# A two-layer decoder trunk on one core: transfers moved to SyncE, gates and transposes given precedence, and seven products in the last gate

## The chip, the core and the metric

The program runs on one core of a Trainium2 chip. A core has five engines, each with its own queue of instructions: TensorE (PE in the profile; its weight loads are PEld), VectorE (DVE), ScalarE (ACT), GpSimd (POOL) and SyncE (SP), which here only issues transfers between memory (HBM) and the core's SBUF. The metric is the device time of one execution in microseconds (us), as the median of several runs. All arithmetic is float32.

## The reference, cut to what matters

The input is h, 256 tokens by 2048 features. Two layers follow, each of the same outline:

```python
hn = rmsnorm(h, norm)
u = hn @ w_in                       # 2048 x 6144, then 2048 x 8208
y = token_mixers(u)                 # gated recurrences (layer 0), mLSTM (layer 1)
h = h + y @ w_out                   # output projection, 2048 x 2048
pl = rmsnorm(p[i] @ ple_w[i], ple_norm[i])
h = h + sigmoid(h @ ple_gate_w[i]) * pl      # the gate, 2048 x 2048
```

and a final `rmsnorm(h, final_norm)` gives the output. The change lies in the output projections and gates of both layers, and in what is loaded and stored around them.

## The kernel before, in words

**A matmul in three.** Every float32 weight tile (128 x 1024, 512 KB) is loaded by SyncE into one of five buffers named raw, and split: ScalarE writes a rounded copy whi (line 137 in `load_weights`, line 219 in `split_weights`), VectorE the rest, wlo = raw - whi (lines 138 and 220). There are four buffers of each. Activations are split the same way (ahl). A product is then three matmuls: high by high, high by low, low by high. Loads, copies and subtractions are written down in the order of the program; a scheduler orders each engine's queue by a priority, which is an instruction's place in the program less an offset (`high_priority`), among those that are ready by its own estimate. Splits have an offset of 400. `issue_after` puts an instruction behind another one of its engine.

**Projections.** With tokens as output rows, a weight matrix is done in chunks of 512 output features, each in four quarters of the 2048 inputs (`quarter_tok`, lines 199 to 213: 24 matmuls, both halves of the tokens, two weight tiles). `project_two` does two chunks interleaved, in the order of quarters (0,0), (0,1), (1,0), (1,1), (0,2), (1,2), (0,3), (1,3), so that the last features are needed late. `plain` is the same quarter in another form.

**Seven products.** `seven` (line 287) does a pair of chunks with one quarter of the inputs (two in some places) as a 2 x 2 block product in seven multiplications in place of eight (Strassen-Winograd). It needs sums of blocks of weights, added by VectorE in place (line 306) or by an accumulating transfer of GpSimd (line 310), and sums of blocks of activations (`combos`, line 247). The other quarters of the pair run as `plain`, between the products, in the order of a string: a and b are plain quarters of the first and second chunk, the digits are products, A and F hand over finished halves, and a dot is a pump. The output projections of both layers ("eo", "oo") and the first gate ("g0") do chunks 0 and 1 by `project_two` and then chunks 2 and 3 by `seven` (`two_and_seven`). The last gate ("g1") does chunks 0 and 1 by `project_two` (through `chunks`, with n = 3), chunk 2 by `project_tok` and chunk 3 by `last_chunk`, in which the second half of the tokens is done in two halves of columns, for a short end.

**What hangs on a finished chunk.** `out_proj` (line 588) adds a finished half to h (VectorE, line 595, offset 100). `ple_gate` (line 601) takes a tanh on ScalarE and two operations on VectorE (lines 608 to 610). Both then start `to_features` (line 553): two 32 x 32 block transposes on VectorE (line 558), a hop through memory issued by GpSimd (`across`, lines 677 and 680: one transfer out, four back), and the split of the features for the next projection (ahl). Such steps are generators in named lanes. Each plain quarter pumps once in its middle: every lane takes a step, and what it issues is put behind the latest instruction noted for its engine (`last`). `ready` runs a lane on until the features that a quarter needs exist.

**Transfers beside the weights.** After the first gate, h (four tiles of 512 KB) is spilled to memory by GpSimd (`spill`, line 1152: six pumps of waiting, then one tile at each), because its room is needed. Before the second output projection it is reloaded by GpSimd (`home`, line 1446: three pumps of waiting, then one tile at each); `out_proj` needs it there. The row of gains of the second layer's embedding norm is loaded by GpSimd in two halves (`row`, line 535), spread over all partitions; `ple_gain_squares` (line 1475) takes squares at its steps 0 to 3 and multiplies by the row at its steps 2 to 5. The row of the final norm is loaded in the same way at the second pump of the last gate.

Of the kernel before, what the change touches and what calls it, by code (L numbers as in the profile page):

```python
# [11 lines left out]
F32 = mybir.dt.float32  # L12
# [7 lines left out]
P = 128  # L20
# [25 lines left out]
def trunk(ctx: ExitStack, tc: tile.TileContext, a, out):  # L46
# [79 lines left out]
    def load_weights(src, pieces=(1, 1), halves=(0, 1), rooms=None):  # L126
        parts = []
        for hf in halves:
            raw = wp.tile([P, 1024], F32, name="raw", tag="raw", bufs=5)
            hi, lo = rooms(hf) if rooms else (wp.tile([P, 1024], F32R, name=n, tag=n) for n in ("whi", "wlo"))  # L130
            n = 1024 // pieces[hf]
            for c in range(0, 1024, n):
                r, h, l = (x[:, c:c + n] for x in (raw, hi, lo))
                sy.dma_start(out=r, in_=block(src, hf * 1024 + c, n))
                with ExitStack() as order:
                    order.enter_context(tc.high_priority(offset=400))
                    last["act"] = s.copy(h, r).ins  # L137
                    last["dve"] = v.tensor_tensor(out=l, in0=r, in1=h.bitcast(F32), op=ALU.subtract).ins  # L138
            parts.append((hi, lo))
        return parts  # L140
# [19 lines left out]
    def tokens(x, k, hf):  # L160
        return x[:, k, hf * P:(hf + 1) * P]

    def project_tok(w, j, act, before=None):

        ps = [pm.tile([P, 512], F32, name="mm", tag="mm") for _ in range(2)]
# [18 lines left out]
        for j in range(2, n):  # L184
            yield project_tok(w, j, act)

    def two_and_seven(w, act, before, where, places, home=None):

        qs = {}
        start("combos", combos(act, 0, qs, *where))  # L190
        for c, ps in enumerate(project_two(w, act, before)):
            for hf in range(2):
                yield c, hf, ps[hf]
        drain("combos")
        for b, hf, src in seven(w, 2, act, qs, (0,), *places(), home and home()):
            yield 2 + b, hf, src

    def quarter_tok(w, j, kq, act, ps):

        parts = load_weights(w[4 * j + kq])  # L200
        for hf in range(2):
            for kk in range(4):
                k = kq * 4 + kk
                hi, lo = parts[kk // 2]
                c = (kk % 2) * 512
                ah, al, _ = act[k // 2]
                xh, xl = (tokens(x, k % 2, hf) for x in (ah, al))
                wh, wl = hi[:, c:c + 512], lo[:, c:c + 512]
                te.matmul(ps[hf], xh, wh, start=(k == 0), stop=False)  # L209
                te.matmul(ps[hf], xh, wl, start=False, stop=False)  # L210
                last["pe"] = te.matmul(ps[hf], xl, wh, start=False, stop=(k == KT - 1)).ins  # L211
            if hf == 0:
                pump()

# [69 lines left out]
    def seven(w, j, act, qs, kqs, room, part, home=None, order=None, acc=None, before=None, third=None):  # L284
# [4 lines left out]
        def load(tile_of, b, side):  # L289
            tiles = []  # L290
            for kq in kqs:
                t = tile_of()
                sy.dma_start(out=t, in_=src(b, side, kq))
                tiles.append(t)
            return tiles

# [32 lines left out]
        E = px.tile([P, 512], F32, name="mx", tag="mx")  # L329
        A, F, B = (pm.tile([P, 512], F32, name="mm", tag="mm") for _ in range(3))  # L330
        b5, g = part(), part()
        X = load(room, 0, 0)
# [12 lines left out]
        if not acc:  # L345
            W = load(ring, 1, 0)
            add(Y, W)
            add(W, X)
        rows = [list(rest), list(rest)]
        did = set()  # L350
        for op in order or ORDERS[len(kqs)]:
            if op in "ab":
                b = "ab".index(op)
                kq = rows[b].pop(0)
                plain(w, j + b, kq, act, ((A, F), (E, B))[b], end=not rows[b])
            elif op == "5":
                product(B, combo(1), split(W))
                add(X, Y)
                if acc:
                    add_loaded(Y)  # L360
                keep(b5, B)
# [165 lines left out]
    def ple_norm(pls, pss, rp):  # L527
# [4 lines left out]
        v.tensor_scalar(rp, rsqrt_cols(total(pss, 4)), 0.5, None, op0=ALU.mult)  # L532
        yield

    def row(pool, tag, bufs, i):

        halves = []
        for b in range(2):
            t = pool.tile([P, 1024], F32, name="row", tag=tag, bufs=bufs)
            gp.dma_start(out=t, in_=a["rows"][i, b * 1024:(b + 1) * 1024].partition_broadcast(P))  # L540
            halves.append(t)
        return halves

    def ple_gain(pls, load):
        rows = load()
# [7 lines left out]
    def to_features(h, c, act, gain, name, more=None):  # L553

        w = room("w")
        w5 = w.rearrange("p (j c h t) -> p h c j t", j=4, c=4, h=2)
        for hf in range(2):
            v.transpose(w5[:, hf], h[:, hf].rearrange("p (c j q) -> p c j q", c=4, j=4))
        r = room("r")
        yield from across(w, r, f"d{name}{c}", 7 if c == 2 else 6)  # L560
        r5 = r.rearrange("p (i c h t) -> p c h i t", i=4, c=4, h=2)
# [23 lines left out]
                step(f"{lane}{kq}")  # L585
        return before

    def out_proj(hq, parts, lane):

        act = {}  # L590
        for c, hf, src in parts:
            drain("home")
            if src is not None:
                with tc.high_priority(offset=100):
                    v.tensor_tensor(out=hq[c][:, hf], in0=src, in1=hq[c][:, hf], op=ALU.add)
            if hf:
                start(f"{lane}{c}", to_features(hq[c], c, act, None, lane))
# [3 lines left out]
    def ple_gate(hq, parts, pls, rp, hss, gain, lane, more):  # L601

        nxt = {}
        for c, hf, src in parts:
            drain("pg")
            th = tp.tile([P, 512], F32, name="th", tag="th")
            h = hq[c][:, hf]
            s.activation(th, src, AF.Tanh, scale=0.5)
            v.scalar_tensor_tensor(th, th, 1.0, pls[c][hf], op0=ALU.add, op1=ALU.mult)
            v.scalar_tensor_tensor(h, th, rp[:, hf:hf + 1], h, op0=ALU.mult, op1=ALU.add)  # L610
# [572 lines left out]
    with tc.tile_pool(name="m1", bufs=2) as m1:  # L1183
# [260 lines left out]
        hq = []  # L1444

        def home():
            for _ in range(3):
                yield
            for c in range(4):
                t = hp.tile([P, 2, 512], F32, name="hq", tag="h")  # L1450
                gp.dma_start(out=t, in_=away[c])
                hq.append(t)
                yield

# [18 lines left out]
            v.tensor_scalar(rp, rsqrt_cols(total(pss, 4)), 0.5, None, op0=ALU.mult)  # L1473

        def ple_gain_squares():
            rows = row(m1, "vt", 6, 1)
            for g in range(6):
                for hf in range(2):
                    if g < 4:
                        squared(pls[g][hf], pss[:, g, hf:hf + 1])  # L1480
                    if g > 1:
                        pl = pls[g - 2][hf]
                        v.tensor_tensor(out=pl, in0=pl, op=ALU.mult,
                                        in1=rows[(g - 2) // 2][:, (g % 2) * 512:(g % 2 + 1) * 512])
                yield

        step("fm3")
# [4 lines left out]
        act = out_proj(hq, two_and_seven(a["oo"], y, ready(y, "fm"), (m1, "vt", 6), in_m1, lambda: hq[3][:, 0]), "fo")  # L1492
        drain("emb")


        hss = m1.tile([P, 5, 2], F32, name="hss", bufs=1)
# [14 lines left out]
                v.scalar_tensor_tensor(sq, pl, 1.0, pl, op0=ALU.mult, op1=ALU.mult, accum_out=o)  # L1511

        def final_rows():
            yield
# [4 lines left out]
        for g, ps in enumerate(chunks(a["g1"], 3, act, ready(act, "fo"))):  # L1519
            drain("fnr")  # L1520
            for hf in range(2):
                pl = pls[g][hf]
                gated(g, ps[hf], hq[g][:, hf], pl, hf)
                v.tensor_tensor(out=pl, in0=pl, in1=fnr[g // 2][:, (g % 2) * 512:(g % 2 + 1) * 512], op=ALU.mult)


        def last_chunk():
# [187 lines left out]
```

## Time and profile before

| what | us |
|---|---|
| median of 3 runs | 1023.46 (1023.36 to 1025.24) |
| the profiled execution | 1024.17 |
| its span, from the first instruction to the last | 1022.4 |

The granted clock of TensorE was 0.997 over the span. The kernel moves 242.66 MB at a mean of 237 GB/s. In the chain of waits, the stages lie about like this (start in us): output projection of layer 0, its seven products 343.5; first gate, its seven products 429.2; second output projection about 839, its seven products 883.1; last gate about 925; last matmul about 1013.

How to read the rows: a row of a timeline has the start, the duration, the engine, the line of the kernel, the operation, the tiles as out<-in, the shapes and how many instructions are merged (x2). The chain that ended last is followed back from the last instruction, and its rows have start, length and what it was. A row of the waits has who waited, for whom, and the total, the number and the longest. A row of stretches has the bounds, then the busy time of PE, PEld, DVE, ACT and POOL with their numbers of instructions, then the clock, the share of the DMA engines and GB/s. "SPq" is SyncE issuing; its duration in a merged row is the stretch over which it issued.

### The profile page before, as it was taken

The numbers are of one execution on the slowest core, as the hardware profiler recorded it, in microseconds if no ns is written. First come the engines' busy times: TensorE is split into PE (matmuls) and PEld (weight loads), VectorE is DVE, ScalarE is ACT, GpSimd is POOL, SyncE is SP. The second block draws the span as 40 slices with busy tenths as digits, with TensorE's granted clock in tenths as the row PEclk, the third lists the DMA queues.
The fourth block names the chain that finished last, engine by engine and source line by source line (L and its number), as shares of the span: only waits on it lengthen the run. The fifth ranks groups of instructions, "written<-read, shape, count | busy, mean of one in ns | idle before, by whom it ended". The sixth has DMA issues, their size and how long they took to land.

```text
span 1022.4 us, 14498 instructions
## 1 busy us (share of the span) xinstructions
PE 1011.1 (99%) x5164; PEld 838.4 (82%) x5164; DVE 828.8 (81%) x1216; ACT 654.0 (64%) x940; POOL 107.1 (10%) x192
## 2 busy tenths in 40 slices
PE   9999999999999999999999999999999999999996
PEld 8888888888888888887888888888888887888885
DVE  7858968969686888888669997888889996986783
ACT  7775554686974455666557878766667777554662
POOL 0111101011111112021012100000011112112000
PEclk9999999999999999999999999999999999999998
DMA  9987756567689799487789756566979789689652
GB/s 358 334 228 247 223 179 198 170 197 232 234 254 306 240 304 300 150 271 246 252 295 289 246 165 211 184 207 194 277 176 287 228 267 310 204 258 297 206 185 83
DMA packets 69817, 242.66 MB, mean 237 GB/s; under 512 B 9041, under 2 KB 10449, under 8 KB 69745
## 3 DMA queue, kind: packets, MB, share of 16 engines
q1 hardware_dynamic: 54576, 192.84, 57.0%
q0 software_dynamic: 14736, 48.38, 17.6%
q8 instruction: 40, 0.66, 0.3%
q10 hardware_dynamic: 432, 0.52, 0.1%
q14 instruction: 33, 0.26, 0.1%
HBM read 221.78 MB, written 19.92 MB: 236 GB/s over the span
## 4 chain that ended last, share of the span: by engine, by line
PE 95%; DMA 2%; DVE 1%; ACT 1%; issue 0%; POOL 0%; ACTq 0%; DVEq 0%; POOLq 0%
PE mm L233 25%; PE mm L209 15%; PE mm L210 15%; PE mm L211 15%; PE mx L233 7%; PE mx L211 3%; PE mx L210 3%; PE mx L209 3%; PE mm L509 1%; DMA row<-in_rows_dram 1%; PE nu L1339 1%; PE mx L509 1%; PE mm L1540 1%; PE mm L1539 1%; PE mm L1541 1%; DMA r<-dfg 1%
## 5 line engine op out<-in xcount | busy, mean ns | idle before, releaser
L138 DVE TENSOR_TENSOR wlo<-raw,whi 128x1024 fp32r<-128x1024 f32 (+1 forms) x313 | 375.9, 1212 | 115.2 <-ACT whi L137 109.0
L137 ACT CAST whi<-raw 128x1024 fp32r<-128x1024 f32 (+1 forms) x313 | 326.3, 1047 | 219.1 <-PE mm L211 100.0
L210 PE MATMUL mm<-wlo,ahl 128*128 128x512 f32 x704 | 274.3, 390 | 1.0 <-DVE wlo L138 1.0
L209 PE MATMUL mm<-whi,ahl 128*128 128x512 f32 x704 | 275.2, 391 | 0.0
L211 PE MATMUL mm<-whi,ahl 128*128 128x512 f32 x704 | 274.0, 389 | 0.0
L233 PE MATMUL mm<-whi,ahl 128*128 128x512 f32 x636 | 204.8, 390 | 0.0
L210 PEld LDWEIGHTS mm<-wlo,ahl 128*128 128x128 f32 x704 | 132.2, 188 | 28.6 <-DVE wlo L138 1.6
L209 PEld LDWEIGHTS mm<-whi,ahl 128*128 128x128 f32 x704 | 132.1, 188 | 28.0 <-issue 0.4
L211 PEld LDWEIGHTS mm<-whi,ahl 128*128 128x128 f32 x704 | 132.2, 188 | 27.4
L233 PEld LDWEIGHTS mm<-whi,ahl 128*128 128x128 f32 x636 | 119.4, 188 | 24.7
L233 PE MATMUL mm<-wlo,ahl 128*128 128x512 f32 x318 | 123.9, 390 | 0.0
L220 DVE TENSOR_TENSOR wlo<-ch,whi 128x1024 fp32r<-128x1024 f32 x62 | 74.8, 1219 | 11.5 <-ACT whi L219 10.4
L219 ACT CAST whi<-ch 128x1024 fp32r<-128x1024 f32 x62 | 64.7, 1049 | 20.9 <-PE mm L233 11.2
L233 PEld LDWEIGHTS mm<-wlo,ahl 128*128 128x128 f32 x318 | 59.7, 188 | 12.2
L209 PE MATMUL mx<-whi,ahl 128*128 128x512 f32 x160 | 62.2, 389 | 0.0
L210 PE MATMUL mx<-wlo,ahl 128*128 128x512 f32 x160 | 62.2, 389 | 0.0
L211 PE MATMUL mx<-whi,ahl 128*128 128x512 f32 x160 | 62.2, 389 | 0.0
L233 PE MATMUL mx<-whi,ahl 128*128 128x512 f32 x168 | 55.3, 390 | 0.0
L233 PE MATMUL mm<-whi,q 128*128 128x512 f32 x132 | 44.8, 390 | 0.0
L233 PEld LDWEIGHTS mx<-whi,ahl 128*128 128x128 f32 x168 | 31.5, 188 | 6.9 <-ACT xr L566 0.4
L209 PEld LDWEIGHTS mx<-whi,ahl 128*128 128x128 f32 x160 | 30.0, 188 | 6.3
L210 PEld LDWEIGHTS mx<-wlo,ahl 128*128 128x128 f32 x160 | 30.0, 188 | 6.2
(380 smaller groups left out, 1255.0 us busy)
## 6 DMA issues: line engine op xcount, KB each, us to landing
raw<-in_ew_dram SPq DMA_DIRECT2D x64, 512.0 KB, 5.0
raw<-in_g_dram SPq DMA_DIRECT2D x62, 512.0 KB, 4.8
raw<-in_oqk_dram SPq DMA_DIRECT2D x32, 512.0 KB, 5.5
raw<-in_eo_dram SPq DMA_DIRECT2D x30, 512.0 KB, 5.0
raw<-in_oo_dram SPq DMA_DIRECT2D x30, 512.0 KB, 5.5
raw<-in_ov_dram SPq DMA_DIRECT2D x29, 512.0 KB, 4.4
raw<-in_oog_dram SPq DMA_DIRECT2D x24, 512.0 KB, 4.3
raw<-in_oz_dram SPq DMA_DIRECT2D x20, 512.0 KB, 5.2
```

The source lines that it names most:

```text
L137: last["act"] = s.copy(h, r).ins
L138: last["dve"] = v.tensor_tensor(out=l, in0=r, in1=h.bitcast(F32), op=ALU.subtract).ins
L209: te.matmul(ps[hf], xh, wh, start=(k == 0), stop=False)
L210: te.matmul(ps[hf], xh, wl, start=False, stop=False)
L211: last["pe"] = te.matmul(ps[hf], xl, wh, start=False, stop=(k == KT - 1)).ins
L219: last["act"] = s.copy(hi, r).ins
L220: last["dve"] = v.tensor_tensor(out=lo, in0=r, in1=hi.bitcast(F32), op=ALU.subtract).ins
L233: last["pe"] = te.matmul(o, x, y, start=(first and k + i == 0), stop=(end and k == n - 1 and i == 2), skip_group_check=True).ins
L509: last["pe"] = te.matmul(ps[hf][:, o:o + w_], tokens(pact[x], k, hf), (hi, lo)[y][:, k * 512 + o:k * 512 + o + w_], start=(n == mine[0]), ...
L1339: te.matmul(ps[:, 0:n], x[:, i, o:o + P], y[:, b, i], start=(b == 0 and x is sh and y is vh), stop=(b == hf and y is vl))
L1539: te.matmul(o, xh, wh, start=(k == 0), stop=False)
L1540: te.matmul(o, xh, wl, start=False, stop=False)
```

## The change

- SyncE in place of GpSimd issues the spill, the reload and the second layer's norm row. So that a pump puts them behind the weight loads written down before, the latest load of SyncE is noted in `last`. The spill waits five pumps and then takes every second one; the reload waits four pumps. The row's halves are loaded at the first two steps, and multiplied by at steps 4 to 7.
- Transposes of `to_features`, the residual adds of `out_proj` and the gate of `ple_gate` get an offset of 450.
- The last gate does chunks 0 and 1 by `seven`, in the order `LATE`, with one quarter in seven products; the first quarter of chunk 2 stands between its first two products, in two other PSUM banks (`third`), and `project_tok` does the rest of chunk 2. Its combinations of activations are begun within the seven products of the second output projection. The final norm's row waits five pumps.

```diff
-LATE = "a5c6.2a7b4aAF.bb"
+LATE = "a526.a7b4aAF.bb"
...
@@ load_weights, and the same in seven's load
-                sy.dma_start(out=r, in_=block(src, hf * 1024 + c, n))
+                last["sp"] = sy.dma_start(out=r, in_=block(src, hf * 1024 + c, n)).ins
...
@@ project_tok
-        for kq in range(4):
+        ps = begun or [pm.tile([P, 512], F32, name="mm", tag="mm") for _ in range(2)]
+        for kq in range(1 if begun else 0, 4):
...
@@ two_and_seven
         drain("combos")
+        if begin is not None:
+            begin()
...
@@ seven
+        if third is not None:
+            plain(w, j + 2, kqs[0], act, third, (True, True))
         Y = load(room, 1, 1)
         product(E, combo(4), split(Y), home is None)
...
                 kq = rows[b].pop(0)
+                if before is not None:
+                    before(kq)
                 plain(w, j + b, kq, act, ((A, F), (E, B))[b], end=not rows[b])
...
@@ to_features
-        for hf in range(2):
-            v.transpose(w5[:, hf], h[:, hf].rearrange("p (c j q) -> p c j q", c=4, j=4))
+        with tc.high_priority(offset=450):
+            for hf in range(2):
+                v.transpose(w5[:, hf], h[:, hf].rearrange("p (c j q) -> p c j q", c=4, j=4))
...
@@ out_proj
-                with tc.high_priority(offset=100):
+                with tc.high_priority(offset=450):
                     v.tensor_tensor(out=hq[c][:, hf], in0=src, in1=hq[c][:, hf], op=ALU.add)
...
@@ ple_gate
-            s.activation(th, src, AF.Tanh, scale=0.5)
-            v.scalar_tensor_tensor(th, th, 1.0, pls[c][hf], op0=ALU.add, op1=ALU.mult)
-            v.scalar_tensor_tensor(h, th, rp[:, hf:hf + 1], h, op0=ALU.mult, op1=ALU.add)
+            with tc.high_priority(offset=450):
+                s.activation(th, src, AF.Tanh, scale=0.5)
+                v.scalar_tensor_tensor(th, th, 1.0, pls[c][hf], op0=ALU.add, op1=ALU.mult)
+                v.scalar_tensor_tensor(h, th, rp[:, hf:hf + 1], h, op0=ALU.mult, op1=ALU.add)
...
@@ spill
-        for _ in range(6):
+        for _ in range(5):
             yield
         for c in range(4):
             d = dr.tile([P, 2, 512], F32, name=f"dh{c}")
-            gp.dma_start(out=d, in_=hq[c])
+            sy.dma_start(out=d, in_=hq[c])
             away.append(d)
             yield
+            yield
...
@@ home
-            for _ in range(3):
+            for _ in range(4):
                 yield
...
-                gp.dma_start(out=t, in_=away[c])
+                sy.dma_start(out=t, in_=away[c])
...
@@ ple_gain_squares
-            rows = row(m1, "vt", 6, 1)
-            for g in range(6):
+            rows = []
+            for g in range(8):
+                if g < 2:
+                    rows.append(half_row(m1, "vt", 6, 1, g, sy))
                 for hf in range(2):
                     if g < 4:
                         squared(pls[g][hf], pss[:, g, hf:hf + 1])
-                    if g > 1:
-                        pl = pls[g - 2][hf]
+                    else:
+                        pl = pls[g - 4][hf]
...
@@ the second output projection and the last gate
+        act, qs1 = {}, {}
+        out_proj(hq, two_and_seven(a["oo"], y, ready(y, "fm"), (m1, "vt", 6), in_m1, lambda: hq[3][:, 0],
+                                   lambda: start("combos", combos(act, 0, qs1, m1, "vt", 6))), "fo", act)
+        drain("emb", "combos")
...
+        def gates():
+            third = [pst.tile([P, 512], F32, name="st", tag="st") for _ in range(2)]
+            before = ready(act, "fo")
+            yield from seven(a["g1"], 0, act, qs1, (0,), *in_m1(), order=LATE, before=before, third=third)
+            for hf, ps in enumerate(project_tok(a["g1"], 2, act, None, third)):
+                yield 2, hf, ps
```

More of the change, by code (lines that the diff above doesn't have):

```diff
@@ L161, in tokens, with project_tok @@
         return x[:, k, hf * P:(hf + 1) * P]
-    def project_tok(w, j, act, before=None):
-        ps = [pm.tile([P, 512], F32, name="mm", tag="mm") for _ in range(2)]
-        for kq in range(4):
+    def project_tok(w, j, act, before=None, begun=None):
+        ps = begun or [pm.tile([P, 512], F32, name="mm", tag="mm") for _ in range(2)]
+        for kq in range(1 if begun else 0, 4):
             if before is not None:
@@ L185, in chunks, with two_and_seven @@
             yield project_tok(w, j, act)
-    def two_and_seven(w, act, before, where, places, home=None):
+    def two_and_seven(w, act, before, where, places, home=None, begin=None):
         qs = {}
@@ L208, in quarter_tok @@
                 wh, wl = hi[:, c:c + 512], lo[:, c:c + 512]
-                te.matmul(ps[hf], xh, wh, start=(k == 0), stop=False)
-                te.matmul(ps[hf], xh, wl, start=False, stop=False)
-                last["pe"] = te.matmul(ps[hf], xl, wh, start=False, stop=(k == KT - 1)).ins
+                te.matmul(ps[hf], xh, wh, start=(k == 0), stop=False, skip_group_check=True)
+                te.matmul(ps[hf], xh, wl, start=False, stop=False, skip_group_check=True)
+                last["pe"] = te.matmul(ps[hf], xl, wh, start=False, stop=(k == KT - 1), skip_group_check=True).ins
             if hf == 0:
@@ L292, in load @@
                 t = tile_of()
-                sy.dma_start(out=t, in_=src(b, side, kq))
+                last["sp"] = sy.dma_start(out=t, in_=src(b, side, kq)).ins
                 tiles.append(t)
@@ L331, in seven @@
         b5, g = part(), part()
+        rows = [list(rest), list(rest)]
         X = load(room, 0, 0)
@@ L348, in seven @@
             add(W, X)
-        rows = [list(rest), list(rest)]
         did = set()
@@ L533, in ple_norm, with half_row @@
         yield
+    def half_row(pool, tag, bufs, i, b, on=gp):
+        t = pool.tile([P, 1024], F32, name="row", tag=tag, bufs=bufs)
+        on.dma_start(out=t, in_=a["rows"][i, b * 1024:(b + 1) * 1024].partition_broadcast(P))
+        return t
     def row(pool, tag, bufs, i):
[L537 to L542, printed above, removed]
+        return [half_row(pool, tag, bufs, i, b) for b in range(2)]
     def ple_gain(pls, load):
@@ L586, in ready, with out_proj @@
         return before
-    def out_proj(hq, parts, lane):
-        act = {}
+    def out_proj(hq, parts, lane, act=None):
+        act = {} if act is None else act
         for c, hf, src in parts:
@@ L1480, in ple_gain_squares @@
                         squared(pls[g][hf], pss[:, g, hf:hf + 1])
-                    if g > 1:
-                        pl = pls[g - 2][hf]
+                    else:
+                        pl = pls[g - 4][hf]
                         v.tensor_tensor(out=pl, in0=pl, op=ALU.mult,
-                                        in1=rows[(g - 2) // 2][:, (g % 2) * 512:(g % 2 + 1) * 512])
+                                        in1=rows[(g - 4) // 2][:, (g % 2) * 512:(g % 2 + 1) * 512])
                 yield
@@ L1513, in final_rows @@
         def final_rows():
-            yield
+            for _ in range(5):
+                yield
             fnr.extend(row(m1, "vt", 6, 2))
@@ L1518, in trunk @@
         warm = tp.tile([P, 1], F32, name="warm", tag="warm", bufs=1)
-        for g, ps in enumerate(chunks(a["g1"], 3, act, ready(act, "fo"))):
+        def gates():
[4 more added lines that the diff above has]
+                yield 2, hf, ps
+        for g, hf, src in gates():
             drain("fnr")
[L1521 to L1524, printed above, removed]
+            pl = pls[g][hf]
+            gated(g, src, hq[g][:, hf], pl, hf)
+            v.tensor_tensor(out=pl, in0=pl, in1=fnr[g // 2][:, (g % 2) * 512:(g % 2 + 1) * 512], op=ALU.mult)
         def last_chunk():
```

2 lines of the change are left out of this document (removed).

## The prediction

> **What bounds the kernel now.** I read the page first, then the waits of the matmul engine, then the chain that ended last, and last the timelines of VectorE where the chain leaves that engine.
>
> ```profile
> span 1022.4 us, 14498 instructions
> ## 1 busy us (share of the span) xinstructions
> PE 1011.1 (99%) x5164; PEld 838.4 (82%) x5164; DVE 828.8 (81%) x1216; ACT 654.0 (64%) x940; POOL 107.1 (10%) x192
> ```
>
> ```profile
> PE mm L210 <- DVE wlo L138: 1.0, 1, 1.0
> ```
>
> TensorE (PE) is busy for 99% of the span, and its longest wait of all is 1.0 us. So a microsecond that any other engine saves is worth nothing, unless it takes away one of PE's few stalls; and a microsecond by which a weight split comes too late is paid in full. Here is where the chain shows that:
>
> ```profile
> 346.25 21.76 PE mm L233 x96
> ...
> 431.97 19.22 PE mm L233 x84
> ...
> 454.58 6.39 DMA r<-dfg
> ...
> 462.55 1.24 DVE wlo L138
> 463.83 1.42 PE mx L233 x5
> ...
> 847.29 11.40 DMA row<-in_rows_dram
> 859.33 0.61 DVE pl L1483
> ...
> 885.84 21.94 PE mm L233 x96
> ```
>
> The first row gives the price of a matmul: 21.76 / 96 = 0.227 us from start to start (their own durations overlap). The chain leaves PE in the middle of the program at only two places. At 463.83 a split (L138) was late behind the features of the first gate, which waited for a hop through memory (r<-dfg); the split takes 1.24, and I put PE's loss at 0.6, what is left of 463.83 - 462.55 = 1.28 when the usual start to start of two or three matmuls is taken off. At 859 VectorE waited for the norm row (row<-in_rows), and the split behind it was late: the 1.0 of the waits, 1.2 with the shortened pace of the next matmul.
>
> **The seven products.** The last gate's first pair does one of its four quarters in seven products in place of eight. Each product is 6 matmuls (2 feature tiles by 3 terms), a plain quarter of two chunks is 48, seven products are 42: 6 x 0.227 = **-1.36**. The third chunk's first quarter only moves. Three more splits, four adds, three subtractions and the second set of combinations come to VectorE, and copies to ScalarE. What hides them is the room in that stage:
>
> ```profile
> 936.00:947.00 11.00, 11.00 (x50) 9.13 (x49) 6.24 (x8) 5.54 (x9) 2.71 (x5) 1.00 0.96 322
> ```
>
> VectorE is busy for 6.24 of 11 us and ScalarE for 5.54. The extra work of VectorE is 3 splits + 4 adds at about 1.2 and 3 subtractions at 0.7, some 10.5 us over a stage of 65 (12 quarters of 24 x 0.227 = 5.4); the room is (11 - 6.24) / 11 of that. I cost it at nothing; without cover it is a rival below.
>
> **Norm rows and reload on SyncE.** The row is now issued in two halves at two pumps, and is used from the fourth pump after the first on. What its place on SyncE means is read from SyncE's own queue:
>
> ```profile
> 821.25 44.93 SPq L134 DMA_DIRECT2D raw<-in_oo_dram  x16
> ```
>
> It issues one weight tile in 44.93 / 16 = 2.8 us, from 821.25 on, so the first half goes out behind the fourth tile, near 832, where GpSimd issued both at 847.29, behind a reload. With the same 11.40 to landing it is there at 844, and first used after 860. The wait at 859 goes: **-1.2** (at least 0, at most 1.2). What is late next there is nothing that I see: the reloads follow at pumps 5 to 8, behind the tiles 10 to 14, about 849 to 860, and h is first added after 872. Queued behind each are weight loads that run 18 us ahead (821.25 against a first use near 839.6). The spill moves in the same way and takes GpSimd out of the way of the hops; no PE stall of the profile hangs on it, so 0. In all SyncE issues 10 transfers more, and the other engines nothing.
>
> **Gates and transposes ahead of the splits.** This is where I differ from "nothing". By the code an instruction's claim is its place in the program less its offset. The splits and the adds of the seven products have 400; gates and transposes had none, the residual adds of the output projection 100, and all get 450. So where they come due while VectorE is full, they now go first. They come due exactly at the start of a group of seven, when the two chunks before it end. The stage of the first gate, on VectorE, with PE's need of the next plain tile at 431.97:
>
> ```profile
> 423.87 2.45 DVE L220 TENSOR_TENSOR wlo<-ch,whi 128x1024 fp32r<-128x1024 f32 x2
> 426.23 0.69 DVE L609 SCALAR_TENSOR_TENSOR th<-th,pl 128x512 f32<-128x512 f32 x1
> 426.84 1.22 DVE L306 TENSOR_TENSOR ch<-ch,raw 128x1024 f32<-128x1024 f32 x1
> 427.97 0.74 DVE L610 SCALAR_TENSOR_TENSOR hq<-th,rp,hq 128x512 f32<-128x512 f32 x1
> 428.63 1.22 DVE L306 TENSOR_TENSOR raw<-raw,ch 128x1024 f32<-128x1024 f32 x1
> 429.77 2.35 DVE L138 TENSOR_TENSOR wlo<-raw,whi 128x1024 fp32r<-128x1024 f32 x2
> ...
> 435.45 0.70 DVE L558 STREAM_TRANSPOSE w<-hq 128x512 f32<-128x512 f32 x1
> 436.08 1.25 DVE L609 SCALAR_TENSOR_TENSOR th<-th,pl 128x512 f32<-128x512 f32 x2
> ```
>
> ```profile
> 443.12 1.29 DVE L558 STREAM_TRANSPOSE w<-hq 128x512 f32<-128x512 f32 x2
> ```
>
> VectorE has no gap from 423.87 on, and the first of the two splits at 429.77 is done at 429.77 + 1.18 = 430.95, 1.0 ahead of PE's 431.97. Behind it lie a transpose (435.45), the two halves of the next chunk's gate (436.08, and two hq steps of 0.74 each after them) and that chunk's transposes (443.12): 0.70 + 1.25 + 1.48 + 1.29 = 4.7 us, all of which may now stand ahead of that split. All of it ahead: 4.7 - 1.0 = 3.7 of stall. Only what is ready before the chunk's second half ends (one transpose, half the gate, one transpose: 0.70 + 0.62 + 0.74 + 0.65 = 2.7): 1.7. I take **+3.0**, nearer the upper end: the split also waits behind the add at 428.63, which the gate pushes too, and by then the second half's tanh is done. The second split has the same need 1.36 later and costs nothing more.
>
> The output projection of the first layer, with PE's need at 346.25:
>
> ```profile
> 344.19 2.35 DVE L138 TENSOR_TENSOR wlo<-raw,whi 128x1024 fp32r<-128x1024 f32 x2
> ```
>
> ```profile
> 349.91 0.68 DVE L595 TENSOR_TENSOR hq<-mx,hq 128x512 f32<-128x512 f32 x1
> 350.51 1.29 DVE L558 STREAM_TRANSPOSE w<-hq 128x512 f32<-128x512 f32 x2
> ```
>
> Split done at 345.37, 0.9 ahead; pulled in front of it 0.68 + 1.29 = 1.97, so 1.07; between 0.5 (one transpose stays behind) and 1.1 I take **+1.0**. The output projection of the second layer, need at 885.84:
>
> ```profile
> 884.04 2.35 DVE L138 TENSOR_TENSOR wlo<-raw,whi 128x1024 fp32r<-128x1024 f32 x2
> ```
>
> Done at 885.22, 0.6 ahead; the same 1.97 would cost 1.35. But the norm's chain of small operations now comes later and makes room before it, so between 0 and 1.4, and **+1.0**, as in the other layer.
>
> On the good side the first gate's hop starts some ten microseconds sooner (its transposes stood at 443.12), so the late split at 462.55 is in time: **-0.6** (0 to 0.6).
>
> **Sum.** -1.36 - 1.2 - 0.6 + 1.0 + 3.0 + 1.0 = +1.84, with ends of -0.96 (-1.36 - 1.2 - 0.6 + 0.5 + 1.7 + 0) and +4.84 (-1.36 + 0 + 0 + 1.1 + 3.7 + 1.4). The profiled execution took 1024.17, its span 1022.4 and 1.77 around it; so 1026.0, and as the median of the runs (1023.46) is 0.71 under that execution, **1025.3**. Ends of this case: 1022.5 and 1028.3. A measurement of this kernel can tell about 0.2%, 2.05 us (1021.4 to 1025.5).
>
> **Rivals.**
>
> *The starts of the sevens hold.* The order on VectorE changes less than I say, or the slack of the tiles behind takes it up. Then the gain stands: -1.36 - 1.2 - 0.6 = -3.16, 1020.3 (1021.4 with one small stall of 1.1). For it: gates that come due in the middle of a seven already run at once without harm. Against it: at all three places the split is under 1.1 us ahead and VectorE has no gap.
>
> *The last gate runs short.* Its start is tighter than before. The pair needed the third quarter of features after 4 plain quarters' halves, 96 matmuls, now after 6 + 24 + 6 + 24 + 18 = 78, so 4.1 us sooner; the stage starts at 883.1 + 186 x 0.227 = 925.3 (883.1: two products of 1.36 ahead of 885.84), so the need is at 943.0.
>
> ```profile
> 938.63 1.43 DVE L575 TENSOR_TENSOR ahl<-r,ahl 128x256 fp32r<-128x256 f32 x4
> ```
>
> These features were ready at 940.1: 2.9 ahead, and three products in a row (5, 2, 6) want three splits and an add, 4.8 us of VectorE, within 4.1 of PE. If the 1.43 of features falls among them, PE waits 4.8 + 1.43 - 4.1 = 2.1. On top of the forecast, 1027.4. It decides once the features end later than 943.0. Against it: the transposes go sooner, and so does the hop.
>
> *Weights behind the reloads: slower.* Four reloads and two half rows go into the queue of the weights.
>
> ```profile
> 850.00:861.00 11.00, 10.25 (x46) 8.15 (x44) 3.95 (x5) 9.74 (x21) 1.06 (x2) 1.00 1.02 379
> ```
>
> Here the engines of the DMA are full (share 1.02, 379 GB/s) and 512 KB take 1.4 us; four of them 5.5, against a lead of 18 us. By the rows this costs 0; it would cost up to 5.5 (1030.8 with the forecast) if the lead were used up. [...] No row of this trace shows a reload in the weights' queue.
>
> **How the numbers follow.** The three stalled starts 0.60: of it 0.33 within the bound, 0.26 above, 0.01 below. The starts hold 0.28: 0.26 below the bound, 0.02 within. The last gate short 0.08, above but for 0.01. Weights behind reloads 0.04, 0.03 of it above. So faster 0.27, same 0.37, slower 0.36. The range runs from 1020.2, just under the rival that keeps the gain, to 1027.2, which leaves out the last gate's case, the reloads and the top of the forecast's own range: some 0.17 together.
>
> **What would show it.** Right: PE has 6 matmuls less (5158); no wait on a row near 860; PE waits for L138 of 2 to 3.7 us near 432 and of about 1 near 346 and 885, with the L558 and gate rows now in front of those splits; no late split at 463. Wrong: the same L138 rows near 432 still ahead of the gate's second half, or ahead of PE by over 1 us (then the sevens hold); a wait inside 925 to 990, on a split or on the features (the last gate); a raw<-in_oo wait of ScalarE between 850 and 885 (reloads).

## The result, and the profile after

The changed kernel takes 1032.99 us as the median of 5 runs (1032.72 to 1033.91) against 1023.36 for the kernel before beside it: 9.6 us slower, a ratio of 1.0093 with a 95% interval of 1.0079 to 1.0108. The profiled execution took 1032.95.

The page of the changed kernel, and who PE waited for (total, times, longest, in us):

```profile
span 1031.2 us, 14514 instructions
## 1 busy us (share of the span) xinstructions
PE 1013.2 (98%) x5158; PEld 838.8 (81%) x5158; DVE 844.2 (82%) x1234; ACT 660.9 (64%) x949; POOL 101.4 (10%) x182
```

```profile
PE mm L235 <- DVE wlo L138: 4.8, 3, 3.0
PE mx L235 <- DVE q L266: 3.5, 1, 3.5
...
PE mm L212 <- DVE wlo L138: 0.4, 1, 0.4
```

PE has the 6 matmuls less, and yet its busy time has not fallen (1013.2 against 1011.1). The kernel before had two waits in the middle of 1.2 us in all; this one has four, of 8.3. Three are for splits and one is for q, a combination of activations. (The 0.4 is at 16.7 us, among the first weights.) (Lines have moved: 233 is now 235, 306 is 308, 558 is 566, 595 is 603, 609 and 610 are 618 and 619.)

The three waits for splits are the three starts of seven products that the prediction named. VectorE's timeline at the first gate, after:

```profile
428.30 0.75 DVE L619 SCALAR_TENSOR_TENSOR hq<-th,rp,hq 128x512 f32<-128x512 f32 x1
428.96 0.68 DVE L618 SCALAR_TENSOR_TENSOR th<-th,pl 128x512 f32<-128x512 f32 x1
429.56 0.70 DVE L566 STREAM_TRANSPOSE w<-hq 128x512 f32<-128x512 f32 x1
430.19 0.71 DVE L619 SCALAR_TENSOR_TENSOR hq<-th,rp,hq 128x512 f32<-128x512 f32 x1
430.82 1.22 DVE L308 TENSOR_TENSOR ch<-ch,raw 128x1024 f32<-128x1024 f32 x1
431.95 0.68 DVE L618 SCALAR_TENSOR_TENSOR th<-th,pl 128x512 f32<-128x512 f32 x1
432.56 1.22 DVE L308 TENSOR_TENSOR raw<-raw,ch 128x1024 f32<-128x1024 f32 x1
433.69 0.74 DVE L619 SCALAR_TENSOR_TENSOR hq<-th,rp,hq 128x512 f32<-128x512 f32 x1
434.35 1.30 DVE L566 STREAM_TRANSPOSE w<-hq 128x512 f32<-128x512 f32 x2
435.57 2.31 DVE L138 TENSOR_TENSOR wlo<-raw,whi 128x1024 fp32r<-128x1024 f32 x2
```

Before, the splits (L138) came right behind the second add (L306), at 429.77. Now gate operations and transposes stand in front of both adds and of the splits, which begin at 435.57. PE's start to start across that wait is 3.43 us where 0.23 is usual: a stall of 3.2. At 346.5 and 890.3 it is 1.28 and 1.24, stalls of 1.05 and 1.01, behind an added residual and two transposes.

The fourth is in the last gate. PE's timeline and VectorE's:

```profile
938.11 0.40 PE L235 MATMUL mx<-wlo,q 128*128 128x512 f32 x1
942.02 0.88 PE L235 MATMUL mx<-whi,q 128*128 128x512 f32 x2 [3.51 <-DVE q L266]
942.70 0.63 PE L235 MATMUL mx<-wlo,q 128*128 128x512 f32 x1
```

```profile
932.15 0.68 DVE L603 TENSOR_TENSOR hq<-mm,hq 128x512 f32<-128x512 f32 x1
932.75 1.21 DVE L222 TENSOR_TENSOR wlo<-ch,whi 128x1024 fp32r<-128x1024 f32 x1
933.88 0.70 DVE L566 STREAM_TRANSPOSE w<-hq 128x512 f32<-128x512 f32 x1
934.51 1.18 DVE L308 TENSOR_TENSOR ch<-ch,raw 128x1024 f32<-128x1024 f32 x1
935.62 1.21 DVE L138 TENSOR_TENSOR wlo<-raw,whi 128x1024 fp32r<-128x1024 f32 x1
936.75 1.22 DVE L308 TENSOR_TENSOR raw<-raw,ch 128x1024 f32<-128x1024 f32 x1
937.88 1.22 DVE L138 TENSOR_TENSOR wlo<-raw,whi 128x1024 fp32r<-128x1024 f32 x1
939.02 1.22 DVE L308 TENSOR_TENSOR ch<-ch 128x1024 f32<-128x1024 f32 x1
940.15 1.22 DVE L222 TENSOR_TENSOR wlo<-raw,whi 128x1024 fp32r<-128x1024 f32 x1
941.29 0.68 DVE L266 TENSOR_TENSOR q<-qc,q 128x512 fp32r<-128x512 f32 x1
```

The second product of the last gate's seven needs q (L266). That operation takes 0.68 us and has no offset, so it stands behind three adds and three splits with 400 that are needed later than it. Start to start across the wait is 3.91: a stall of 3.7.

And the matmuls behind the two long stalls are slow. Stretches of 4 us; the sixth column is the granted clock of PE:

```profile
437.00:441.00 4.00, 4.00 (x11) 3.11 (x11) 4.00 (x4) 0.00 (x0) 0.93 (x2) 0.57 0.91 312
441.00:445.00 4.00, 4.00 (x19) 3.27 (x18) 1.52 (x2) 2.10 (x2) 1.26 (x3) 1.00 0.95 288
...
942.00:946.00 4.00, 3.98 (x10) 3.13 (x11) 2.44 (x5) 1.04 (x1) 0.00 (x0) 0.57 0.99 251
946.00:950.00 4.00, 4.00 (x19) 3.29 (x18) 1.53 (x5) 2.32 (x5) 0.00 (x0) 1.00 0.72 287
```

Over the 4 us behind each, the granted clock is 0.57, and PE has 11 and 10 matmuls where it has 19 in the next 4 us. Most come 0.427 us apart, where 0.227 is usual; that costs 1.6 and 1.7 (7 of them each time with 0.2 more, and the matmuls just beside them with 0.1 more). Stalls and slow matmuls make 1.2 + 4.8 + 1.1 at the three starts and 5.4 in the last gate, 12.5 us. The last gate's last tanh stands at 1023.09 where it stood at 1013.26, 9.8 later.

### The profile page after: what moved, and what is told of

It reads as the page before. It is cut to its first block, busy times and chain, and to the rows that moved or that the text cites. A ratio compares the mean times of both kernels' runs of the same rounds, so it can differ in the third digit from the quotient of the medians.

```text
span 1031.2 us, 14514 instructions
## 1 busy us (share of the span) xinstructions
PE 1013.2 (98%) x5158; PEld 838.8 (81%) x5158; DVE 844.2 (82%) x1234; ACT 660.9 (64%) x949; POOL 101.4 (10%) x182
## 4 chain that ended last, share of the span: by engine, by line
PE 93%; DVE 3%; ACT 1%; issue 1%; DMA 1%; ACTq 0%; DVEq 0%
PE mm L235 28%; PE mm L211 14%; PE mm L212 14%; PE mm L213 14%; PE mx L235 8%; PE mx L211 2%; PE mx L213 2%; PE mx L212 2%; PE nu L1349 1%; DMA raw<-in_pw_dram 1%; PE mm L515 1%; PE mm L1563 1%; PE mm L1562 1%; PE mm L1561 1%; DVE wlo L138 1%
## 5 line engine op out<-in xcount | busy, mean ns | idle before, releaser
L138 DVE TENSOR_TENSOR wlo<-raw,whi 128x1024 fp32r<-128x1024 f32 (+1 forms) x309 | 371.6, 1212 | 111.7 <-ACT whi L137 105.4
L211 PE MATMUL mm<-whi,ahl 128*128 128x512 f32 x640 | 250.3, 392 | 0.0
L212 PE MATMUL mm<-wlo,ahl 128*128 128x512 f32 x640 | 249.4, 390 | 0.4 <-DVE wlo L138 0.4
L213 PE MATMUL mm<-whi,ahl 128*128 128x512 f32 x640 | 249.1, 389 | 0.0
L235 PE MATMUL mm<-whi,ahl 128*128 128x512 f32 x720 | 233.6, 393 | 0.0
L235 PEld LDWEIGHTS mm<-whi,ahl 128*128 128x128 f32 x720 | 136.5, 190 | 28.5
L235 PE MATMUL mm<-wlo,ahl 128*128 128x512 f32 x360 | 141.7, 394 | 4.8 <-DVE wlo L138 4.8
L211 PEld LDWEIGHTS mm<-whi,ahl 128*128 128x128 f32 x640 | 120.1, 188 | 25.4 <-issue 0.4
L213 PEld LDWEIGHTS mm<-whi,ahl 128*128 128x128 f32 x640 | 120.1, 188 | 25.1
L222 DVE TENSOR_TENSOR wlo<-ch,whi 128x1024 fp32r<-128x1024 f32 x67 | 81.0, 1220 | 12.8 <-ACT whi L221 11.2
L221 ACT CAST whi<-ch 128x1024 fp32r<-128x1024 f32 x67 | 70.0, 1050 | 24.7 <-PE mm L235 12.2
L235 PE MATMUL mx<-whi,ahl 128*128 128x512 f32 x192 | 63.2, 390 | 0.0
L211 PE MATMUL mx<-whi,ahl 128*128 128x512 f32 x128 | 49.8, 389 | 0.0
L212 PE MATMUL mx<-wlo,ahl 128*128 128x512 f32 x128 | 49.8, 389 | 0.0
L213 PE MATMUL mx<-whi,ahl 128*128 128x512 f32 x128 | 49.8, 389 | 0.0
L235 PE MATMUL mm<-whi,q 128*128 128x512 f32 x144 | 49.1, 390 | 0.0
L235 PEld LDWEIGHTS mx<-whi,ahl 128*128 128x128 f32 x192 | 36.0, 188 | 7.9 <-issue 0.4
L235 PE MATMUL mx<-wlo,ahl 128*128 128x512 f32 x96 | 37.4, 389 | 0.0
L235 PEld LDWEIGHTS mm<-whi,q 128*128 128x128 f32 x144 | 27.0, 188 | 5.7
```

The source lines that it names most:

```text
L211: te.matmul(ps[hf], xh, wh, start=(k == 0), stop=False, skip_group_check=True)
L212: te.matmul(ps[hf], xh, wl, start=False, stop=False, skip_group_check=True)
L221: last["act"] = s.copy(hi, r).ins
L222: last["dve"] = v.tensor_tensor(out=lo, in0=r, in1=hi.bitcast(F32), op=ALU.subtract).ins
L235: last["pe"] = te.matmul(o, x, y, start=(first and k + i == 0), stop=(end and k == n - 1 and i == 2), skip_group_check=True).ins
```

## The experiments

Theory A, formed on these rows: all of the loss comes from the offsets of 450 and what they do to the order on VectorE. Rival B: the transfers moved to SyncE hold weights up. Rival C: the last gate's pair is too tight by itself. Runs of the kernel before lay beside each.

**Old offsets.** The changed kernel without the three offsets.

```diff
@@ to_features, ple_gate
-        with tc.high_priority(offset=450):
@@ out_proj
-                with tc.high_priority(offset=450):
+                with tc.high_priority(offset=100):
```

> The changed kernel with the offsets of transposes, residual adds and gates back as before the change (none, 100, none). Theory A (the order on VectorE): the offsets alone cost the time. Away go the stalls at 346, 433 and 890 with the slow matmuls behind them (1.2 + 4.8 + 1.1) and, because the transposes no longer stand ahead of the last combination (q) of the last gate, its wait at 938 with the slow matmuls behind it (5.4): 1033.0 - 12.5 = 1020.5, plus 0.6 if the late split near 466 comes back. Rival B (the transfers on SyncE hold up weights): within 1 us of 1033.0. Rival C (the last gate's wait is the seven products' own and not the offsets'): 1033.0 - 7.1 = 1025.9, with PE still waiting some 3.5 us for q near 931.

Measured: 1020.72 (before: 1022.70; ratio 0.9981, interval 0.9973 to 0.9990). All 12 us are gone, with the last gate's wait among them; B and C fall. All that PE waited for:

```profile
PE st L99 <- PEq L1726: 0.8, 1, 0.8
PE mx L515 <- ACT whi L484: 0.4, 1, 0.4
```

Both are in the first microseconds of the program. The q of the last gate, on VectorE's timeline of this run, with what stands around it:

```profile
924.57 0.69 DVE L602 TENSOR_TENSOR hq<-mm,hq 128x512 f32<-128x512 f32 x1
925.17 1.22 DVE L222 TENSOR_TENSOR wlo<-ch,whi 128x1024 fp32r<-128x1024 f32 x1
926.30 0.69 DVE L266 TENSOR_TENSOR q<-qc,q 128x512 fp32r<-128x512 f32 x1
926.91 1.22 DVE L308 TENSOR_TENSOR ch<-ch,raw 128x1024 f32<-128x1024 f32 x1
```

With the old offsets it stands just ahead of the adds, behind the same residual add and the same split as in the changed kernel. There, at 933.88, a transpose stood in its place, and q came only behind the block of instructions with an offset. The run takes all three offsets back; that it was the transposes' is read from the order of these rows, and no run sets them apart in the last gate.

**Combinations ahead.** The changed kernel with all its offsets, and 450 for the last gate's combinations too.

```diff
@@ combos, called with ahead=450 for the last gate alone
+        def early():
+            return tc.high_priority(offset=ahead) if ahead else ExitStack()
...
-            s.copy(q[:, 0:512], c)
-            v.tensor_tensor(out=q[:, 512:1024], in0=c, in1=q[:, 0:512].bitcast(F32), op=ALU.subtract)
+            with early():
+                s.copy(q[:, 0:512], c)
+                v.tensor_tensor(out=q[:, 512:1024], in0=c, in1=q[:, 0:512].bitcast(F32), op=ALU.subtract)
```

> The changed kernel with an offset of 450 for the combinations of the last gate too; all else as it is. Theory A: only the wait for q near 938 and the slow matmuls behind it go, 3.7 + 1.7 = 5.4: 1027.6; the stalls at 346, 433 and 890 stay as they are. Rival B: no change, 1033.0. If the last gate is held by its features as well: between 1028 and 1031, with another wait in the first 20 us of the last gate.

Measured: 1027.56 (1.0039, 1.0026 to 1.0051), 5.4 below the changed kernel as expected. The wait for q is gone, and the three waits for splits are there:

```profile
PE mm L235 <- DVE wlo L138: 4.8, 3, 3.0
```

That the time agrees to the tenth has luck in it. The runs go from 1025.5 to 1028.2, and in the profiled one (1028.23) PE waited 1.8 us for a rounded copy (whi) at the start of the program and had no slow matmuls behind the stall at the first gate.

**Both.** Old offsets and combinations ahead.

> Both: old offsets for transposes, adds and gates, and 450 for the combinations of the last gate. Theory A: all four stalls go, 1020.5 (1021.1 if the late split near 466 comes back), so 2.3 to 2.9 faster than the kernel before the change: 1.4 from six matmuls less and 1.2 from the norm row. Rival B: 1033. Rival C: also 1020.5, and then faster than the run with old offsets alone by 5.

Measured: 1020.27 (0.9977, 0.9968 to 0.9987). The intervals of this run and of the one with old offsets alone overlap: once the old offsets are back, the combinations need no help. Both beat the kernel before. In the profiled execution, one of the longest of these runs (1022.24), PE waited 1.8 us at 461 for the hop of the first gate's features (r<-dfg), and the late split behind it was there, at 465. So that split can be late with the change, too.

**Only the offsets.** The kernel before with the three offsets and nothing else of the change.

> The kernel before the change with nothing but the offsets of 450 for transposes, adds and gates. Theory A: 1.2 + 4.8 + 1.1 = 7.1 more than before at the three starts of seven products, less 0.6 for the late split near 464: 1029.9; the last gate has no seven products here and does not stall, and the wait on the norm row near 860 stays or is hidden. Rival B (transfers): 1023.4. Rival C says the same as A here.

Measured: 1029.68 (1.0061, 1.0048 to 1.0074). So the offsets alone cost about 7, with no transfer moved and no product changed; B falls a second time. PE waits for splits 4.8 us in three places here too, and matmuls are slow behind the stall at the first gate (clock 0.60 from 437 to 441, 12 matmuls).

**Only SyncE.** The kernel before with the spill, the reload and the norm row on SyncE (the diff is the change's own, for those parts).

> The kernel before the change with nothing but the SyncE part: spill, reload and norm row issued by SyncE at the new pumps, the row multiplied two steps later. Theory A: the wait for the norm row near 860 goes, -1.2 (0.12%), nothing else moves; the late split near 464 stays: 1.2 below the runs of the kernel before beside it. Rival B (transfers in the weights' queue hold weights up): slower by up to 5.5, with ScalarE waiting for raw tiles between 850 and 885.

Measured: 1021.61 (0.9988, 0.9979 to 0.9997), 1.2 below. PE waits for nothing behind the first microsecond, so weights are not held up. Where the 1.2 lies is looked at under the last run.

**Only the seven products.** The kernel before with the last gate's new pair, its combinations and the later final row.

> The kernel before the change with nothing but the seven products in the last gate (with their combinations and the later final row). Theory A: six matmuls less, -1.4, if the combinations are in time; the wait near 860 and the late split near 464 stay. Rival C (the pair is too tight by itself): PE waits near 931 for q or for features, 1 to 5 slower than that.

Measured: 1020.63 (0.9977, 0.9969 to 0.9986): 2.2 below, the interval from 1.4 to 3.2, where 1.4 was expected. PE waits for nothing in the last gate; C falls a second time.

**Gates and adds alone**, and **transposes alone**: the kernel before with 450 on the one or on the other.

> The kernel before the change with the offset of 450 on the gates of the first gate and on the residual adds, not on the transposes. Theory A (work pulled ahead of a split costs what exceeds the split's slack): at the first gate 1.3 + 1.3 of gate operations come ahead of two splits that have 1.0 and 1.3 of slack: 0.9 to 1.6; at the output projections one add of 0.6 against 0.9 and 0.6: nothing. So 0.9 to 1.6 above the kernel before, and no slow matmuls. A rival in which each pulled operation costs its own time: 2.6 + 2 x 0.6 = 3.8.

> The kernel before the change with the offset of 450 on the transposes alone. Theory A: a chunk's transposes can't go before its gate or add, which keep their old places, so only one transpose of 0.6 comes ahead at the first gate, within the slack of 1.0: no stall at the starts of the seven products, the same time as before (0 to -0.6). The rival in which each pulled operation costs its own time: the transposes' share of the 7.1, that is about 3 (eight transposes of 0.6, less nothing).

Measured: 1023.91 (1.0008, 0.9999 to 1.0017), 1.1 above (the interval just takes in no change), and 1022.57 (0.9996, 0.9987 to 1.0005), the same as before. In the first, the splits at the first gate cost PE 0.8 and 0.3 (start to start 0.99 and 0.54); nothing is late at the output projections. In the second no split is late. The parts make 1.1 and -0.2 and together they make 7 (1.6 of it slow matmuls): about the first 1.0 us of what is pulled ahead is free, and transposes can't go ahead until what they read has.

**Transposes twice.** The kernel before with all three offsets, and each pair of transposes written twice over.

```diff
-            for hf in range(2):
+            for hf in (0, 1, 0, 1):
                 v.transpose(w5[:, hf], h[:, hf].rearrange("p (c j q) -> p c j q", c=4, j=4))
```

> The kernel before the change with all three offsets of 450, and the transposes of the output projections and gates done twice over (the second pass writes the same again). Theory A: four more transposes of 0.63 stand ahead of the late split at each of the three starts, 2.5 each, less what room lies before: stalls near 346, 433 and 890 of 1.0, 3.2 and 1.0 grow by 1.5 to 2.5 each, so 4.5 to 7.5 above the run with the offsets alone (1029.7): 1034 to 1037. On the slow matmuls: at the first gate, with a stall of about 5.5, some eight at 427 ns again; at 346 and 890, with stalls of 2.5 to 3.5, none or some; if a short pause is enough to slow the clock, slow matmuls at all three, and 3 us more. A theory in which the order alone matters and not the work: 1029.7.

Measured: 1038.14 (1.0146, 1.0129 to 1.0163), 8.5 above the run with the offsets alone (7.9 when each is taken against the kernel before beside it), 1 over the range. The stall at the first gate grew by 2.4 (start to start 5.79 against 3.43), those at the output projections by 1.3 each, and a split at 411 came to be late by 0.8, which I had not seen coming. These make 5.8; more slow matmuls make the rest, some 2. On the clock, stretches behind the stalls at 346, 435 and 895 (columns as above):

```profile
350.00:354.00 4.00, 4.00 (x18) 3.31 (x19) 3.44 (x4) 1.05 (x1) 0.00 (x0) 1.00 1.02 307
435.00:441.00 6.00, 0.67 (x3) 0.19 (x2) 6.00 (x9) 3.58 (x7) 2.79 (x5) 0.79 0.44 155
441.00:445.00 4.00, 3.94 (x9) 3.14 (x10) 4.00 (x5) 0.00 (x0) 1.08 (x2) 0.50 0.90 294
895.00:899.00 4.00, 1.98 (x8) 1.05 (x6) 4.00 (x7) 1.81 (x2) 2.75 (x5) 1.00 0.67 204
899.00:903.00 4.00, 3.98 (x11) 3.16 (x11) 3.76 (x6) 0.00 (x0) 0.00 (x0) 0.57 1.02 326
```

The clock is slow behind two of the three, and two stalls of the same size (start to start 2.24 at 347.7 and 2.25 at 896.8) differ: full clock behind the one, 0.57 behind the other.

**Before, again.** The same program as before, for a second profile.

> The kernel before the change once more, for a second profile. If PE's two stalls in the middle (the late splits near 464 and 860) belong to the order of the instructions, they are there again with 0.6 and 1.2; if they hang on how long transfers take in a run, one or both are gone, and the span is that much shorter.

Measured: one run of 1022.33, span 1020.6. Neither stall is there. VectorE at the norm row, and all that PE waited for:

```profile
853.42 1.29 DVE L1483 TENSOR_TENSOR pl<-pl,row 128x512 f32<-128x512 f32 x2 [2.31 <-DMA row<-in_rows_dram]
854.63 2.35 DVE L138 TENSOR_TENSOR wlo<-raw,whi 128x1024 fp32r<-128x1024 f32 x2
```

```profile
PE st L99 <- PEq L1706: 0.8, 1, 0.8
PE mx L509 <- ACT whi L478: 0.5, 1, 0.5
```

VectorE waits for the row here too, but 2.3 us where the first profile had 7.0, and then the split is not late. In the profiles of the seven products alone and of the transposes alone it waits 4.5 and 2.3, and PE feels nothing there either. The wait belongs to the program; that PE felt it belongs to that one execution.

So the 1.2 of the SyncE part need not be this stall, and the second profile shows another place for it. The last gate's last tanh stands at 1011.41 here and at 1011.36 with SyncE alone: PE has gained nothing. The span is shorter all the same, 1019.4 against 1020.6, because the last store of the output lands sooner. The transfers of the last 9.6 us, here and with SyncE alone (the last number of a store is the time from issue to landing):

```profile
q14 instruction: 1, 0.01, 0.6%
...
out_dram<-pl SPq DMA_DIRECT2D x1, 512.0 KB, 3.7
```

```profile
out_dram<-pl SPq DMA_DIRECT2D x1, 512.0 KB, 2.8
```

In all five profiles with these transfers on SyncE that store takes 2.8, and in all seven without 3.2 to 4.0. In these seven a packet of the kind that the profile calls "instruction" (q14) runs among the last stores, and in the five none does. Whether that packet is the cause no run shows. With the seven products alone the last tanh comes at 1010.01, 1.40 sooner than here, which is the six matmuls; its last store takes 3.2, and its span (1018.5) is 2.0 shorter.

## Why the prediction was wrong

**The three starts** were right. The prediction had stalls of 1.0, 3.0 and 1.0; measured were 1.05, 3.2 and 1.01, through the work it named, at the places it named. The lower end for the first gate (1.7, the second half of the gate behind the split) did not come: that half was ready and went first. All seven operations that I listed went ahead. Counted from start to start they take 4.35 and not the sum of their durations, 4.7, since each starts a little before the one ahead ends; 4.35 less the 1.0 of slack is 3.3. At the second output projection the size has luck in it: the rows gave 1.35, and I took 1.0 for room that the norm's chain would make, but before the change no operation of that chain stood in the 6 us ahead of that split.

**Slow matmuls** were left out. The step "(so much work) less (so much slack) is the stall" stops at the end of the stall. Behind the long ones, of 3.2 and 3.7, PE runs slow for 3 to 4 us (granted clock 0.57 over 4 us, most matmuls 0.427 us apart): 1.6 at the first gate and 1.7 in the last, 3.3 of the miss. No row of the profile before could show it, since PE never stopped there for over 1.2 us behind its start, and the clock is 1.00 from 462 to 470 and from 857 to 865, at and behind its two stalls. Nor would the size of a stall alone have told that the term was due: with combinations ahead the same stall of 3.2 at the first gate has no slow matmul behind it (clock 1.00).

**The last gate** is the step that failed: "I cost it at nothing". It was argued from VectorE's share of busy time over the stage (6.24 of 11 us), and a share says nothing of the order. The stall there measured 3.7, with 1.7 of slow matmuls behind it: 5.4 in place of nothing. The combinations have no offset, and they come due among six instructions of one stage with 400. The rival that I wrote down for this stage had the right place and the wrong piece: features in place of combinations, 2.1 in place of 3.7, chance 0.08. What I missed is an interplay inside the change: the seven products alone cost nothing here, as I had it, but the transposes that I had moved in my sum at the earlier sevens also move here, and take from the combinations the little room that they had. The run with combinations ahead and the run with old offsets each take this wait away, so it takes both: the offsets of 450, and a combination without one. Which of the offsets it is rests on the order of the rows.

**The gains of -1.2 and -0.6** were read from one execution. In the second profile of the same program both stalls are absent, and that span is 1.8 shorter. The sum may even have counted part of this twice: it took both stalls off the profiled time, and then took off 0.71 more to come to the median. That the run with SyncE alone gained 1.2 (interval 0.3 to 2.1), as forecast, is luck: in its profile the gain is at the end of the program, where I had no term, and not at the norm row.

**The six matmuls** were counted right (5158), and they are worth the 1.36: with the seven products alone the last tanh comes 1.40 sooner than in the second profile of the kernel before. The run as a whole gained more (2.2, from 1.4 to 3.2), and in its profile what goes beyond lies behind the last tanh, 0.6. In the profiles this is also why the parts do not add up to the whole (the medians have 1.2 and 2.2 apart and 2.0 together, from 1.0 to 2.8, in the run with old offsets). From the last tanh to the end they have about 9.1 in the kernel before, 8.5 with the seven alone, and 8.1 both with SyncE alone and with old offsets: the two parts shorten the same end, which can be shortened once.

**Weights behind the reloads** did not happen, in the changed kernel or with SyncE alone: PE waits for nothing between 850 and 885 in the one, and for nothing behind the first microsecond in the other.

So with the terms as the profiles have them: 7.1 at the starts and 5.4 in the last gate, both with their slow matmuls, and the wait of 0.4 among the first weights, less 1.36 and less 1.1 at the end, is 10.4. Against the second profile of the kernel before the span is 10.6 longer. Against the first, in which the kernel before had its two stalls of 1.8, the terms make 8.6 and the spans differ by 8.8. The medians differ by 9.6. Without the offsets the change would have been a gain of 2.0 us; that run, the one with both edits and the one with the seven products alone, 1020.3 to 1020.7, are the best of this study.

## What to carry to other kernels

Where one engine is full, an instruction may go ahead of another only as far as the other's slack: list, for each split, when it ends and when it is used, and add up what comes in front of it; the excess is the stall. Here about the first microsecond was free and the rest was not. Whoever gives one kind of work precedence should look at everything without precedence that is due in the same stretch, for a small operation with a near need can end up behind a block with a far one; a share of busy time does not show this. Profile a kernel twice before a stall of a microsecond is booked as a gain. And when a gain of the expected size comes, look whether it is at the expected place: when the last matmul runs, and how long the end takes after it.

## What the runs showed of the hardware

A pause of PE can cost more than itself. In the profiles of the changed kernel and of the offsets alone a pause of 3.2 us was followed by some eight matmuls at 427 ns; in the profile with combinations ahead the same pause, 3.43 start to start, was followed by none:

```profile
435.00:439.00 4.00, 1.04 (x5) 0.51 (x3) 4.00 (x6) 3.77 (x8) 2.77 (x5) 1.00 0.38 113
439.00:443.00 4.00, 3.94 (x17) 3.29 (x18) 4.00 (x5) 0.00 (x0) 0.64 (x2) 1.00 0.87 283
```

The clock stays at 1.00, and the second 4 us have 17 matmuls. So whether the clock falls is not settled by the length of the pause alone. The pauses of 1.05 and 1.01 us of the changed kernel did not bring it down (1.00 from 346 to 354 and from 890 to 898); those of 3.7 and 5.6 did (0.57 and 0.50 over 4 us); those of 3.2 did in two of three profiles (0.57 and 0.60 over 4 us). Of three pauses of about 2 in the middle of the program one did (0.57 over 4 us). That one is at 896.8 in the run with transposes twice, where a pause of 0.35 and 1.3 us of matmuls go before it. The same two pauses at 347.7 did not (1.00 from 350 to 354), nor did the wait of 1.8 at 461 in the run with both edits (clock 1.00 from 459 to 467). Why a pause of 2.0 was enough once and one of 3.2 once was not, these runs do not show.
